# A two-layer trunk kernel: the causal mask of DeltaNet's decays written by transfers, GpSimd's powers read a step later, the first heads' gated rows beside the next units, and the first loads in another order

## The chip, the cores and the metric

The kernel runs on one core of one Trainium2 chip, as one launch. The metric is the device time of that core in microseconds (us), the median of several runs. TensorE is called PE here, VectorE DVE, ScalarE ACT, GpSimd POOL and SyncE SP, as in the profile; "SPq" and "POOLq" are the DMA issues of the last two.

## What is computed

The reference is a trunk of two layers over 256 tokens of width 1024, in fp32:

```python
# each layer
x = x + 0.5 * swiglu(rmsnorm(x, ffn1_norm), ffn1_w_in, ffn1_w_out)   # 1024 -> 2 x 2816 -> 1024
x = x + mixer(rmsnorm(x, mix_norm))      # layer 0: attention and RG-LRU; layer 1: DeltaNet
x = x + cross_attention(rmsnorm(x, xa_norm), rmsnorm(mem, xa_mem_norm), ...)
x = x + 0.5 * swiglu(rmsnorm(x, ffn2_norm), ffn2_w_in, ffn2_w_out)
# after both layers
out = rmsnorm(x, final_norm)

# the DeltaNet mixer, 8 heads of width 128, chunks of C = 64 tokens
qkv, z, a, b = split(h @ w_in)
q, k, v = split(silu(causal_dwconv(qkv, conv_w)))       # 4 taps
q, k = l2norm(q), l2norm(k)
beta = sigmoid(b);  g = -exp(a_log) * softplus(a + dt_bias)
gcum = cumsum(g)                                         # within a chunk
decay = exp(where(tril, gcum[i] - gcum[j], -inf))        # the causal mask of the decays
amat = I + strict_lower((k * beta) k^T * decay)          # inverted, then u, w, states and outputs
o = rmsnorm(chunked outputs, o_norm) * silu(z)
out = o @ w_out
```

The kernel works in chunks of 128 tokens, two of them, instead of 64.

## The kernel before

**Weights.** fp32 products are made of three fp32r products of high and low halves. All weights pass through one stream: `plan` lists units of 1024 (or fewer) rows by 256 columns, and `queue` lists their halves of four 128-row pieces, 512 KB each. `load_to` issues a half's DMA into one of five buffers `raw` (`RAW = 5`, SP's queue, L135). `split_half` makes the high half on ACT (L148, a copy to fp32r) and the low half on DVE (L149, a subtraction). `unit` multiplies: for each of 8 row pieces and two column halves `mm3` issues a high product of 512 columns (L190, both halves of the activations `x2`) and a low one of 256 (L194). A unit is thus 16 such pairs on PE. `unit` yields after each quarter and `run` or `fill` then calls `tick`, which splits the next half and runs what is due: `after(n, fn)` puts a step n ticks later. `w` issues loads until five halves beyond the last split one are under way. The order of the instructions on each engine then comes from the framework's scheduler, except in `manual_schedule` blocks, where it is the order of the code.

**Start (`setup`).** x is loaded in six DMAs into two of the five `raw` buffers (L462), in the order of its columns: 256, 256 and 512 columns, for both token halves each. Then come three halves of weights. PE turns x by transposes (`transposed`, L419, eight for each of two banks `psf` and `pss`, four 256-column pieces), and `take` makes the high half on ACT (L481) and the low on DVE (L484). The first norm's scale is not applied here but to the results of the first units (`times_bc`). The rows of `x` are squared on ACT (L492) and copied to `xT` on DVE (L494). `ffn` then runs the units of the first SwiGLU: the first unit goes to `gs`, the second to `us`, and so on; the first unit's 16 pairs need two halves of weights, and so do the second's.

**DeltaNet (`mixer1`).** The units of its input product run in the order of `DN_ORDER`: k, q, v and z of head pairs 0 to 3 (`k0` to `z3`), `K2` and `K3` being keys of the cross-attention. `conv` adds a unit's bank to `xn` (ACT L260, DVE L261: this frees the bank) and runs the taps on DVE (L1026); `silu` follows. `01|v3 z1` means that `back(0)` and `back(1)`, the inverse and the outputs of pairs 0 and 1, run in alternation with the units v3 and z1, `DN_FILL` telling after how many quarters.

The decays of pair p: `decay_rows` writes gcum to DRAM (POOL's DMA `gd<-gt`, L1010), `load` reads it into `e` on every partition (POOL's DMA `e<-gd`, L1068, four of 256 KB), `masked` adds on POOL the mask `neg_up` (`dn_negup`, -1e30 above the diagonal; L1072, four additions of 128x512), and `exp` is on ACT. `DEC = (2, 4, 4)` are the ticks of the three. `matrix` multiplies `kk`, `nb` and `e` to `na` on DVE (L1120), which goes to DRAM for the inversion (`store`, `invert`).

`sums` takes a norm's power of -0.5 on POOL (`rs_dn`, L331). `scales` then makes on DVE `nb_all` (L1098, from a reciprocal on DVE) and `hb_all` (L1099, from `rs_dn`), `products` makes `rq_all` (L1146, from `rs_dn`) and the decayed scores (L1150). `rq_all` is read in `back` alone and `hb_all` in the v units' rows.

At the end of a group `gated` multiplies each pair's outputs on DVE (L1286, four of 128x128; their norm is POOL's `ro`, then `ro_all` L1279), and `gated_T` turns them on PE (L1295) into `a2`, the input of the output product. In the first group this stands between the background units and `v2`.

## Time and profile before

| what | value |
|---|---|
| median of 3 runs | 1262.11 us (1261.82 to 1263.52) |
| the profiled execution | 1262.28 us, its span 1260.5 us |
| PE busy | 1240.2 us (98%) |
| DVE busy | 936.8 us (74%) |
| ACT busy | 748.9 us (59%) |
| POOL busy | 86.1 us (7%) |
| moved by DMA | 221.86 MB, 176 GB/s |

The span is that of the profiled core from its first to its last instruction; what lies around it is 1.8 us in this execution. "Busy" adds up instructions, so that the rest of PE's span, some 20 us, is time in which it waited or had nothing. Times of the timeline are counted from the span's start. The layer-1 DeltaNet mixer lies at about 795 to 910 us.

### The profile page before, as it was taken

The page shows a single profiled execution, that of the slowest core. Times are in us where ns is not written, and L with a number is a line of the kernel's source. Part 1 is how long each engine was busy: PE and PEld are TensorE (multiplying, and loading weights), DVE is VectorE, ACT ScalarE, POOL GpSimd, SP SyncE. Part 2 cuts the span into 40 slices and gives each one's busy share as a digit, 9 for nine tenths or more (in the row PEclk, how much of TensorE's full clock was granted, in tenths as well). Part 3 has the DMA queues.
Part 4 walks back from the last instruction along what each step waited for, and adds up shares of the span by engine and source line. Part 5 has one row for each costly group of instructions (what it writes and reads, how often), then busy time and mean ns, then how long its engine had stood idle before and what let it go on. Part 6 is the DMA issues. An engine that isn't in the chain of part 4 may idle for free.

```text
span 1260.5 us, 20362 instructions
## 1 busy us (share of the span) xinstructions
PE 1240.2 (98%) x7726; PEld 1107.8 (88%) x7726; DVE 936.8 (74%) x1595; ACT 748.9 (59%) x1274; POOL 86.1 (7%) x101
## 2 busy tenths in 40 slices
PE   7999999999999999999999999999999999999998
PEld 6888889888998888888888888888898998888887
DVE  6888866788668778766877756999757768777753
ACT  5766645876555665545655545775747555665543
POOL 1000020000101000011000001130001101000000
PEclk9999999999999999999999999999999999999999
DMA  7766585644545666567666555656533645666561
GB/s 231 234 209 194 183 253 184 182 151 133 185 134 153 187 195 186 174 192 232 185 187 184 190 184 176 176 161 174 138 102 105 196 134 155 186 195 185 178 194 63
DMA packets 228409, 221.86 MB, mean 176 GB/s; under 512 B 14920, under 2 KB 226008, under 8 KB 228184
## 3 DMA queue, kind: packets, MB, share of 16 engines
q1 hardware_dynamic: 227384, 217.42, 55.9%
q0 software_dynamic: 928, 3.15, 0.9%
q8 instruction: 60, 0.98, 0.3%
q14 instruction: 37, 0.30, 0.1%
HBM read 215.03 MB, written 5.51 MB: 175 GB/s over the span
## 4 chain that ended last, share of the span: by engine, by line
PE 74%; issue 17%; DVE 4%; DMA 2%; ACT 1%; POOL 1%; SPq 0%; POOLq 0%; DVEq 0%; ACTq 0%
PE psw L190 16%; PE pss L190 13%; PE psf L190 8%; PE psw L194 8%; PE pss L194 7%; PE psw L232 5%; PE psf L194 4%; PE psf L232 3%; PE pss L232 2%; PE psw L206 1%; DVE wt L149 1%; PE pss L1219 1%; PE psf L1227 1%; PE psw L210 1%; DVE y L1026 1%
## 5 line engine op out<-in xcount | busy, mean ns | idle before, releaser
L149 DVE TENSOR_TENSOR wt<-raw,wt 128x1024 fp32r<-128x1024 f32 (+1 forms) x406 | 484.9, 1198 | 201.7 <-ACT wt L148 199.3
L148 ACT ACTIVATE wt<-raw 128x1024 fp32r<-128x1024 f32 (+1 forms) x406 | 418.1, 1036 | 170.3 <-PE psw L194 57.1
L190 PE MATMUL psw<-x,wt 128*128 128x512 f32 x856 | 308.2, 396 | 3.2 <-DVE xn L261 3.0
L194 PE MATMUL psw<-x,wt 128*128 128x256 f32 x856 | 223.7, 282 | 0.0
L190 PE MATMUL pss<-x,wt 128*128 128x512 f32 x536 | 195.3, 396 | 1.9 <-ACT wt L148 1.9
L190 PEld LDWEIGHTS psw<-x,wt 128*128 128x128 f32 x856 | 159.2, 188 | 31.1 <-DVE xn L261 3.6
L194 PEld LDWEIGHTS psw<-x,wt 128*128 128x128 f32 x856 | 161.2, 189 | 8.5
L194 PE MATMUL pss<-x,wt 128*128 128x256 f32 x536 | 140.2, 282 | 0.5 <-DVE wt L149 0.5
L190 PE MATMUL psf<-x,wt 128*128 128x512 f32 x344 | 124.1, 393 | 0.0
L190 PEld LDWEIGHTS pss<-x,wt 128*128 128x128 f32 x536 | 101.3, 189 | 19.6 <-ACT wt L148 2.3
L194 PEld LDWEIGHTS pss<-x,wt 128*128 128x128 f32 x536 | 101.6, 190 | 6.3 <-DVE wt L149 1.0
L326 POOL TENSOR_TENSOR acc<-acc,sq 128x256 f32<-128x256 f32 x49 | 44.9, 916 | 658.8 <-ACT sq L324 658.5
L194 PE MATMUL psf<-x,wt 128*128 128x256 f32 x344 | 89.5, 281 | 0.0
L190 PE MATMUL pss<-h,wt 128*128 128x512 f32 x242 | 87.0, 397 | 0.0
L190 PE MATMUL psw<-h,wt 128*128 128x512 f32 x242 | 86.9, 396 | 0.0
L190 PEld LDWEIGHTS psf<-x,wt 128*128 128x128 f32 x344 | 64.6, 188 | 11.0
L194 PEld LDWEIGHTS psf<-x,wt 128*128 128x128 f32 x344 | 64.8, 188 | 3.8
L194 PE MATMUL pss<-h,wt 128*128 128x256 f32 x242 | 66.0, 280 | 0.0
L194 PE MATMUL psw<-h,wt 128*128 128x256 f32 x242 | 66.0, 280 | 0.0
L190 PE MATMUL psf<-h,wt 128*128 128x512 f32 x176 | 63.3, 397 | 0.0
L190 PEld LDWEIGHTS pss<-h,wt 128*128 128x128 f32 x242 | 45.5, 188 | 9.9
L190 PEld LDWEIGHTS psw<-h,wt 128*128 128x128 f32 x242 | 45.5, 188 | 9.9
(379 smaller groups left out, 2135.3 us busy)
## 6 DMA issues: line engine op xcount, KB each, us to landing
raw<-in_ffn_w_in_dram SPq DMA_DIRECT2D x176, 512.0 KB, 4.4
raw<-in_ffn_w_out_dram SPq DMA_DIRECT2D x80, 512.0 KB, 4.0
raw<-in_xa_wkv_dram SPq DMA_DIRECT2D x32, 512.0 KB, 3.9
raw<-in_dn_w_in_dram SPq DMA_DIRECT2D x32, 512.0 KB, 4.0
raw<-in_ab_w_in_dram SPq DMA_DIRECT2D x20, 512.0 KB, 4.5
raw<-in_xa_wq_dram SPq DMA_DIRECT2D x16, 512.0 KB, 3.5
raw<-in_xa_wo_dram SPq DMA_DIRECT2D x16, 512.0 KB, 3.6
raw<-in_ffn_w_out_dram SPq DMA_DIRECT2D x16, 256.0 KB, 2.8
```

The costliest lines, as they stand in the source:

```text
L148: nc.scalar.activation(a, r, AF.Copy)
L149: nc.vector.tensor_sub(b, r, a.bitcast(F32))
L190: nc.tensor.matmul(out.rearrange("p a s -> p (a s)"), w[:, 0, cols], mov[:, k].rearrange("p a s -> p (a s)"), start=k == start, stop=k == ...
L194: nc.tensor.matmul(out[:, 0], w[:, 1, cols], mov[:, k, 0], start=False, stop=False)
L206: nc.tensor.matmul(out.rearrange("p a s -> p (a s)"), mov[:, k, 0, tok], w.rearrange("p a s -> p (a s)"), start=k == 0, stop=k == KD - 1)
L210: nc.tensor.matmul(out[:, 0], mov[:, k, 1, tok], w[:, 0], start=False, stop=False)
L232: self.nc.tensor.matmul(out, a[u], b[w], start=first and i == 0, stop=last and i == 2)
L326: (eng or nc.gpsimd).tensor_add(self.acc, self.acc, sq)
L1026: nc.vector.scalar_tensor_tensor(y[:, j, d:], x[:, :S - d], tap(i), y[:, j, d:], op0=OP.mult, op1=OP.add)
L1219: nc.tensor.matmul(py[:, i], na[:, i], tu[:, 0, i], start=True, stop=True)
L1227: nc.tensor.matmul(pp[:, i], l[:, i], r[:, i], start=True, stop=True)
```

## The change

1. **Mask.** `masked` is gone. At tick 2 of the mixer (`MASK`), four DMAs on SP's queue copy `neg_up` into the four `e` buffers (256 KB each, from SBUF to SBUF), and POOL's four DMAs `e<-gd` add to what is there (`accum_op`). `DEC` is `(2, 4)`.
2. **Powers.** `hb_all` and `rq_all` are computed one tick later than `rs_dn`.
3. **Gated rows of pairs 0 and 1.** After the first group they are put 1 to 4 ticks into the next unit, `q2`. Unit v2 moves into the group's background, and one quarter of it runs before the first step of `back`.
4. **Start.** The second half of the first unit and the first half of the second change places in the queue of weights. x has a buffer of its own (`xs`), so that five halves can be loaded at once; its four DMAs stand around those of the first two halves of weights. PE gets 16 idle products of `ones` (7, 3 and 6). The products of both first units with the first half of x are issued before x's second half is turned; the rest comes after it. The first unit's halves of weights are split in two pieces each, and so is the second unit's second half.

On PE, the rows at the start of the program. Before (`ident,raw` are the transposes of x, `x_79` is `x2`, `wt` the split weights):

```order
L466 MATMUL psw<-ident,dcw 128x128
L419 MATMUL psf<-ident,raw 128x128 x4
L419 MATMUL pss<-ident,raw 128x128 x4
L419 MATMUL psf<-ident,raw 128x128 x4
L419 MATMUL pss<-ident,raw 128x128 x4
L190 MATMUL pss<-x_79,wt 128x512
L194 MATMUL pss<-x_79,wt 128x256
L190 MATMUL pss<-x_79,wt 128x512
```

All 16 transposes stand ahead of the first product. After, from the same place (`xs` is x's own buffer, `ones` the idle products' operand):

```order
L491 MATMUL psw<-ones 128x128 x7
L483 MATMUL psw<-ident,dcw 128x128
L429 MATMUL psf<-ident,xs 128x128 x4
L491 MATMUL psw<-ones 128x128 x3
L429 MATMUL pss<-ident,xs 128x128 x4
L491 MATMUL psw<-ones 128x128 x6
L200 MATMUL psw<-x_79,wt 128x512
L204 MATMUL psw<-x_79,wt 128x256
```

Eight transposes stand ahead of the first product now; the other eight come after eight pairs of products.

On POOL, the rows of the first decays in the DeltaNet mixer, where DVE waits for `rs_dn`. Before:

```order
L1010 DMA gd<-gt 16x128
L331 TENSOR_TENSOR rs_dn<-ss,mhalf 128x4
L1068 DMA e<-gd 128x512 x4
L1072 TENSOR_TENSOR e<-e,dn_negup 128x512
L331 TENSOR_TENSOR rs_dn<-ss,mhalf 128x4
L1072 TENSOR_TENSOR e<-e,dn_negup 128x512 x3
L331 TENSOR_TENSOR rs_dn<-ss,mhalf 128x4 x4
```

After:

```order
L1062 DMA gd<-gt 16x128
L341 TENSOR_TENSOR rs_dn<-ss,mhalf 128x4
L1123 DMA e<-gd 128x512 x4
L341 TENSOR_TENSOR rs_dn<-ss,mhalf 128x4 x5
L341 TENSOR_TENSOR ro<-so,mhalf 128x4 x2
```

The four additions are gone, and nothing stands between the DMAs and the next powers.

On DVE, the rows around the second pair's scales in the same place. Before:

```order
L1026 SCALAR_TENSOR_TENSOR y<-xn,dcw,y 128x254
L1098 TENSOR_TENSOR nb_all<-nbeta,r_8264 128x2x2
L1099 TENSOR_TENSOR hb_all<-ss,rs_dn 128x2x2
L1026 SCALAR_TENSOR_TENSOR y<-xn,dcw,y 128x253
L261 TENSOR_TENSOR xn<-psw,xn 128x256
L1120 SCALAR_TENSOR_TENSOR na<-psf,nb_all,e 128x128 x4
```

After:

```order
L1078 SCALAR_TENSOR_TENSOR y<-xn,dcw,y 128x254
L1150 TENSOR_TENSOR nb_all<-nbeta,r_8294 128x2x2
L271 TENSOR_TENSOR xn<-psw,xn 128x256
L1078 SCALAR_TENSOR_TENSOR y<-xn,dcw,y 128x253
L1151 TENSOR_TENSOR hb_all<-ss,rs_dn 128x2x2
L1172 SCALAR_TENSOR_TENSOR na<-psf,nb_all,e 128x128 x2
```

`xn`, which frees PE's bank, stands ahead of `hb_all` and of a tap now.

On DVE, the first group's gated rows. Before:

```order
L1267 TENSOR_TENSOR qk<-pss,q_8348 128x2x128
L1276 TENSOR_SCALAR so<-so 128x4
L1279 TENSOR_TENSOR ro_all<-ro,rq_all 128x2x2
L1286 SCALAR_TENSOR_TENSOR qk<-qk,ro_all,z 128x128 x4
L1276 TENSOR_SCALAR so<-so 128x4
L261 TENSOR_TENSOR xn<-psw,xn 128x256
L1279 TENSOR_TENSOR ro_all<-ro,rq_all 128x2x2
L1286 SCALAR_TENSOR_TENSOR qk<-qk,ro_all,z 128x128 x4
```

After:

```order
L1319 TENSOR_TENSOR qk<-pss,q_8375 128x2x128
L1078 SCALAR_TENSOR_TENSOR y<-xn,dcw,y 128x253
L1328 TENSOR_SCALAR so<-so 128x4
L1331 TENSOR_TENSOR ro_all<-ro,rq_all 128x2x2
L1338 SCALAR_TENSOR_TENSOR qk<-qk,ro_all,z 128x128 x4
L1328 TENSOR_SCALAR so<-so 128x4
L271 TENSOR_TENSOR xn<-psw,xn 128x256
L1331 TENSOR_TENSOR ro_all<-ro,rq_all 128x2x2
L1338 SCALAR_TENSOR_TENSOR qk<-qk,ro_all,z 128x128 x3
```

The multiplications stand in the same succession, with v2's taps ahead of them; on PE, a whole unit (q2) lies around their transposes where before the end of z1 did.

The diff, cut to its core:

```diff
 NEG = -1e30
-DN_ORDER = ('k0 k1 q0 q1 k2 v0 k3 v1 z0', '01|v3 z1', 'v2 q2 q3 z2', '23|z3 K2 K3')
-DN_FILL = ((1, 0, 1, 2, 0, 2, 1, 3, 2, 10, 1), (1, 0, 1, 0, 2, 1, 1, 0, 0, 5, 0))
+DN_ORDER = ('k0 k1 q0 q1 k2 v0 k3 v1 z0', '01|v3 z1 v2', 'q2 q3 z2', '23|z3 K2 K3')
+DN_FILL = ((1, 0, 1, 2, 0, 2, 1, 3, 2), (1, 0, 1, 0, 2, 1, 1, 0, 0, 5, 0))
...
 TWICE = 'k0 k1 q0 q1'.split()
-DEC = (2, 4, 4)
+DEC = (2, 4)
+MASK = 2
...
         self.queue = [(i, k) for i, u in enumerate(self.plan) for k in range(0, u[4], 4)]
+        self.queue[1], self.queue[2] = self.queue[2], self.queue[1]
...
             yield from ffn(2, l)
-    def load_to(self, n):
+    def load_to(self, n, step=4):
...
             src = self.t[name][l, (k0 + k) * P:(k0 + k + m) * P, c0:c0 + cols]
-            nc.sync.dma_start(raw[:, :m, :cols], src.rearrange("(k p) c -> p k c", p=P))
+            src = src.rearrange("(k p) c -> p k c", p=P)
+            for u in range(0, m, step):
+                us = slice(u, min(m, u + step))
+                nc.sync.dma_start(raw[:, us, :cols], src[:, us])
...
             self.n_load += 1
-    def split_half(self):
+    def split_half(self, step=4):
...
         wt = self.p_wt.tile([P, 4, 2, 256], F32R, name="wt")
-        a, b, r = wt[:, :n, 0, :cols], wt[:, :n, 1, :cols], self.raws.pop(self.n_half)[:, :n, :cols]
+        raw = self.raws.pop(self.n_half)
         self.n_half += 1
-        nc.scalar.activation(a, r, AF.Copy)
-        nc.vector.tensor_sub(b, r, a.bitcast(F32))
+        for u in range(0, n, step):
+            us = slice(u, min(n, u + step))
+            a, b, r = wt[:, us, 0, :cols], wt[:, us, 1, :cols], raw[:, us, :cols]
+            nc.scalar.activation(a, r, AF.Copy)
+            nc.vector.tensor_sub(b, r, a.bitcast(F32))
...
         nc.scalar.activation(warm, self.ones[:, :1], AF.Silu)
-        xs = [self.p_raw.tile([P, D], F32, name="raw") for _ in range(2)]
+        x_pool = tc.tile_pool(name="xs", bufs=1, reuse_waits="tile")
+        xs = x_pool.__enter__().tile([P, 2, D], F32, name="xs")
...
         put(rows0, 0, "ffn1_norm", nc.sync, times=8)
-        for a, b in ((0, 256), (256, 512), (512, 1024)):
-            for j in range(2):
-                nc.sync.dma_start(xs[j][:, a:b], x[:, j, a:b])
-        self.load_to(3)
+        for a, b in ((0, 256), (256, 512)):
+            nc.sync.dma_start(xs[:, :, a:b], x[:, :, a:b])
+        self.load_to(1, 2)
+        self.load_to(2)
+        for a, b in ((512, 768), (768, 1024)):
+            nc.sync.dma_start(xs[:, :, a:b], x[:, :, a:b])
+        self.load_to(RAW)
+        xs = [xs[:, j] for j in range(2)]
...
         with tc.manual_schedule():
+            def idle(n):
+                ps = self.bank("w").rearrange("p a s -> p (a s)")
+                for _ in range(n):
+                    nc.tensor.matmul(ps[:, :P], self.ones, self.ones, start=True, stop=True)
+            idle(7)
...
             def take(ks, ps):
-                if ks.start == 6:
-                    self.split_half()
...
                                                    op0=OP.mult, op1=OP.subtract)
-            self.transposed(xs, take)
+            self.first = [[self.bank(w) for w in u] for u in ("ww", "ws")]
+            def products(u, half, j):
+                self.mm3(self.first[u][j], self.halves[u], slice(j * P, j * P + P), self.x2,
+                         range(4 * half, 4 * half + 4))
+            self.transposed(xs, take, (0,))
+            idle(3)
+            self.transposed(xs, take, (1,))
+            idle(6)
+            self.split_half(2)
+            products(0, 0, 0)
             self.split_half()
+            products(0, 0, 1)
+            self.transposed(xs, take, (2, 3))
+            products(1, 0, 0)
+            products(1, 0, 1)
+            for u in range(2):
+                self.split_half(2)
+                for j in range(2):
+                    products(u, 1, j)
+            self.load_to(4 + RAW)
...
                 nc.vector.tensor_copy(self.xT[:, ks], ps)
+        x_pool.__exit__(None, None, None)
         self.acc, self.ms = None, ms
+        self.n_take = 2
...
                 us = hp.tile([P, 2, S], F32, name="us", bufs=2)
-                self.run(self.unit(f"ffn{i}_w_in", c * 256, mov, self.to(gs), lead=c == 0))
-                up = deque([self.unit(f"ffn{i}_w_in", FF + c * 256, mov, self.to(us))])
-                if c == 0:
+                if self.first:
+                    for dst, banks in zip((gs, us), self.first):
+                        for j, ps in enumerate(banks):
+                            self.to(dst)(j, ps)
+                    self.first, up = None, deque()
+                    self.stats_rows()
+                else:
+                    self.run(self.unit(f"ffn{i}_w_in", c * 256, mov, self.to(gs), lead=c == 0))
+                    up = deque([self.unit(f"ffn{i}_w_in", FF + c * 256, mov, self.to(us))])
+                if c == 0 and up:
...
                 e = four("e", EB)
+                def mask():
+                    nc.sync.dma_start(e, neg_up[:, None, :].to_broadcast([P, 4, P]))
...
                     nc.gpsimd.dma_start(e, bass.AP(tensor=gd.tensor, offset=gd.offset + 4 * p * P,
-                                                   ap=[[0, P], [1, 4 * P]]))
-                def masked():
-                    nc.gpsimd.tensor_add(e, e, neg_up[:, None, :].to_broadcast([P, 4, P]))
+                                                   ap=[[0, P], [1, 4 * P]]), accum_op=OP.add)
...
                     st[p]["e"] = e
-                d0, d1, d2 = DEC
+                d0, d1 = DEC
+                self.after(MASK, mask)
                 self.after(n + d0, load)
-                self.after(n + d1, masked)
-                self.after(n + d2, exp)
+                self.after(n + d1, exp)
...
                     nc.vector.tensor_mul(nb, nbeta[:, :, hs], r2)
-                    nc.vector.tensor_mul(hb, ss, r)
+                    self.after(1, lambda: nc.vector.tensor_mul(hb, ss, r))
...
                     ss, r = sums(s.pop("sq"), twice)
-                    nc.vector.tensor_scalar(rq_all[:, :, hs], r, -P ** -0.5, None, op0=OP.mult)
+                    self.after(1, lambda: nc.vector.tensor_scalar(rq_all[:, :, hs], r, -P ** -0.5, None, op0=OP.mult))
...
                     value_steps(c, y, twice)
-            assert AB[0] < AB[1] < AB[2] < min(AB[3:]) and DEC[0] < DEC[1] <= DEC[2]
+            assert AB[0] < AB[1] < AB[2] < min(AB[3:]) and DEC[0] < DEC[1]
...
                 parts = list(DN_FILL[i // 2])
+                if i == 1:
+                    self.fill(bg, 1)
...
                         self.fill(bg, parts.pop(0))
+                if i == 1:
+                    self.fill(bg)
+                    for n, p in enumerate(group):
+                        self.after(1 + n, lambda p=int(p): gated(p))
+                        self.after(3 + n, lambda p=int(p): gated_T(p))
+                    continue
...
                 for p in group:
```

## The prediction

> **What bounds the kernel now.** The page's first part comes first:
>
> ```profile
> span 1260.5 us, 20362 instructions
> PE 1240.2 (98%) x7726; PEld 1107.8 (88%) x7726; DVE 936.8 (74%) x1595; ACT 748.9 (59%) x1274; POOL 86.1 (7%) x101
> ```
>
> PE is the bound, and nothing in the change takes a product away. A gain can come only out of the 20.3 us in which PE isn't busy (1260.5 - 1240.2) and out of products at a low clock. The view of PE's waits lists these 20 us; the lines that the change can touch are:
>
> ```profile
> PE psw L466 <- DMA dcw<-in_ffn_norm_dram: 3.4, 1, 3.4
> PE psw L190 <- DVE xn L261: 3.0, 2, 1.5
> PE pss L190 <- ACT wt L148: 1.9, 1, 1.9
> PE pss L1295 <- DVE qk L1286: 1.6, 2, 1.3
> PE psf L419 <- DMA raw<-in_x_dram: 1.4, 3, 0.9
> PE pss L1219 <- DMA tu<-d: 0.5, 1, 0.5
> PE psw L206 <- DVE ti L1186: 0.3, 1, 0.3
> ```
>
> Two places hold them: the start (3.4 + 1.9 + 1.4) and the DeltaNet mixer (3.0 + 1.6 + 0.5 + 0.3 = 5.4).
>
> **Start.** The timeline of the first 26 us (start, duration, engine and line, tiles, in brackets the idle time and its releaser):
>
> ```profile
> 6.54 0.84 ACT L481 ACTIVATE x<-pss,bc 128x256 fp32r<-128x256 f32 x2 [0.40 <-PE pss L419]
> 7.41 0.88 DVE L484 SCALAR_TENSOR_TENSOR x<-pss,bc,x 128x256 fp32r<-128x256 f32 x2 [0.35 <-ACT x L481]
> 8.87 1.06 PE L419 MATMUL pss<-ident,raw 128*128 128x128 f32 x4
> 10.67 1.06 ACT L148 ACTIVATE wt<-raw 128x1024 fp32r<-128x1024 f32 x1 [0.72 <-DMA raw<-in_ffn_w_in_dram]
> 11.78 0.79 PE L190 MATMUL pss<-x,wt 128*128 128x512 f32 x1 [1.85 <-ACT wt L148]
> 14.06 0.63 PE L190 MATMUL pss<-x,wt 128*128 128x512 f32 x1
> 14.70 0.63 PE L190 MATMUL pss<-x,wt 128*128 128x512 f32 x1
> 14.82 0.68 DVE L494 COPY xT<-psf 128x512 f32<-128x512 f32 x1
> 16.42 0.40 PE L190 MATMUL psf<-x,wt 128*128 128x512 f32 x1
> 16.77 0.39 PE L190 MATMUL psf<-x,wt 128*128 128x512 f32 x1
> 22.15 1.22 DVE L149 TENSOR_TENSOR wt<-raw,wt 128x1024 fp32r<-128x1024 f32 x1
> 25.46 0.39 PE L190 MATMUL psf<-x,wt 128*128 128x512 f32 x1
> ```
>
> The first product waits until 11.78 for the first half of weights, whose DMA lands behind all of x. A pair takes 14.70 - 14.06 = 0.64 us at first and 16.77 - 16.42 = 0.35 later, so that the clock opens between 15.3 and 16.4. The third unit starts at 25.46; that is the mark, since everything behind it is a chain of units. The window of 5 to 11 us (its length, busy PE, PEld, DVE, ACT and POOL with their counts, clock, DMA share, GB/s) shows what the transfers do meanwhile:
>
> ```profile
> 5.00:11.00 6.00, 3.73 (x14) 2.22 (x12) 2.63 (x6) 2.84 (x7) 0.01 (x1) 1.00 0.89 294
> ```
>
> After: x's first half is turned and split as before (ACT ends at 6.54 + 0.84 = 7.38, DVE at 8.29). The first half of weights now stands behind 512 KB of x, not 1 MB. At those 294 GB/s 512 KB less are 1.8 us, and with half a tile to wait for another 0.9: it lands at about 10.6 - 2.7 = 7.9 or, at the rate of the first packets, a little sooner. Half a split is 0.53 on ACT and 0.61 on DVE (halves of the 1.06 and 1.22): first high product at 8.0 to 8.4, first low at about 9. Eight pairs on the first unit are bound by its second piece and end at about 11.6; eight transposes (1.06 for four, cold) give 12.5 to 13.7; 24 pairs at 0.35 are 8.4. That is 20.9 to 22 for the third unit (and 0.2 for the rows of the statistics), if DVE follows. DVE doesn't: x's last four low pieces (2 x 0.88) end at about 14.9, the two remaining splits (1.22 each) at about 17.3, and behind them it has four copies to `xT` (4 x 0.68, from 14.82 on in the row), four sums for `gs` and `us` (half as wide, an estimate of 4 x 0.34) and the 1.22 of the next half: 17.3 + 2.7 + 1.4 + 1.2 = 22.6. The third unit's low products start at about 22.5. Gain: 25.46 - 22.5 = 3.0. Against it: the sixth half of weights can be issued only when a buffer is free (-0.3), and the clock. The 16 idle products may open it before the real ones or not; if not, some four of the pairs until 12 take 0.64 and not 0.35, 1.4 us less. I take 2.0, in the middle between 3.0 - 0.3 = 2.7 and 2.7 - 1.4 = 1.3; ends 0 (as before) and 4.4 (25.46 - 21.1, were DVE no bound).
>
> The Trainium skill, page "TensorE: Matmul & The Clock Gate", Part 1, says that the clock opens after a window of about 3.4 us of activity; the 3.6 to 4.6 us from 11.78 agree. Part 4 says that transposes don't count for it, which speaks against an early opening, since eight of them stand between the idle products; by it the start would give 1.3 instead of 2.7.
>
> **The powers and the mask.** The timeline of the mixer:
>
> ```profile
> 811.68 0.46 DVE L1026 SCALAR_TENSOR_TENSOR y<-xn,dcw,y 128x253 f32<-128x253 f32 x1
> 813.68 0.17 DVE L1099 TENSOR_TENSOR hb_all<-ss,rs_dn 128x4 f32<-128x4 f32 x1 [0.85 <-POOL rs_dn L331]
> 814.25 2.25 POOL L1068 DMA_DIRECT2D e<-gd  x4 [0.60 <-DMA gd<-gt]
> 818.87 1.56 POOL L1072 TENSOR_TENSOR e<-e,dn_negup 128x512 f32<-128x512 f32 x1 [2.37 <-DMA e<-gd]
> 819.21 1.25 DVE L1098 TENSOR_TENSOR nb_all<-nbeta,r 128x4 f32<-128x4 f32 x1
> 820.46 1.28 ACT L1077 ACTIVATE e<-e,ngc 128x128 f32<-128x128 f32 x4 [2.40 <-POOL e L1072]
> 821.41 3.94 POOL L1072 TENSOR_TENSOR e<-e,dn_negup 128x512 f32<-128x512 f32 x3
> 821.46 1.26 DVE L1099 TENSOR_TENSOR hb_all<-ss,rs_dn 128x4 f32<-128x4 f32 x1 [1.01 <-POOL rs_dn L331]
> 822.65 1.56 DVE L1026 SCALAR_TENSOR_TENSOR y<-xn,dcw,y 128x253 f32<-128x253 f32 x1
> 824.60 0.50 PE L190 MATMUL psw<-x,wt 128*128 128x512 f32 x1 [1.46 <-DVE xn L261]
> 829.22 0.17 DVE L1146 TENSOR_SCALAR rq_all<-rs_dn 128x4 f32<-128x4 f32 x1 [0.87 <-POOL rs_dn L331]
> 830.97 0.50 PE L190 MATMUL psw<-x,wt 128*128 128x512 f32 x1 [1.52 <-DVE xn L261]
> ```
>
> While POOL adds the mask, DVE operations with two inputs in SBUF stand still: `nb_all` takes 1.25 and ends with the addition, `hb_all` 1.26 against 0.17 at 813.68, a tap 1.56 against 0.46. That is 1.08 + 1.09 + 1.10 = 3.3 us of DVE, and its waits for `rs_dn` before 824.60 are 0.85 + 1.01; the second of these stands behind POOL's first addition. (The Trainium skill, "SBUF — State Buffer", "Who interferes with whom", calls this an exclusive lock between GpSimd and DVE with two SBUF inputs; the three rows agree, and taking the mask off POOL frees them.) So DVE loses 3.3 + 1.01 = 4.3 us just before 824.60, where PE waits 1.46, and 0.87 more before 830.97, where PE waits 1.52. The 4.3 are more than both waits, and the rest of the backlog goes with it, so both go: 3.0. `xn` stands ahead of `hb_all` in the new order, which alone would save the first. Next late is nothing on DVE by a wait I can see, though it stays nearly full:
>
> ```profile
> 780.00:800.00 20.00, 19.78 (x115) 16.95 (x114) 18.09 (x40) 14.37 (x29) 0.64 (x1) 1.00 0.71 202
> 820.00:840.00 20.00, 17.02 (x110) 14.90 (x109) 17.87 (x37) 16.35 (x37) 7.72 (x7) 1.00 0.60 164
> ```
>
> In 820 to 840 DVE is busy 17.87, some 2.2 of it blocked time; v2's taps come only behind pair 0's inverse. Ends for both waits: 0 and 3.3.
>
> The four mask DMAs are 1.05 MB more on SP's queue early in the mixer, among the loads of `dn_w_in`. At 202 GB/s and a share of 0.71, the engines could carry 285 GB/s; 1.05 MB are 3.7 us of them and 20 x 0.29 = 5.8 are idle. The loads queued behind are late by at most 3.7, and the weights wait in their buffers for longer than that: no wait of ACT for `raw` stands in this stretch. Cost 0; without that cover, 3.7 us at most.
>
> The accumulating DMA has no row. The nearest are:
>
> ```profile
> e<-gd POOLq DMA_DIRECT2D x4, 256.0 KB, 6.0
> tu<-d SPq DMA_DIRECT2D x8, 256.0 KB, 3.9
> ```
>
> From 814.25 to 818.87 the first `e` took 4.6, the median is 6.0. Adding means reading the destination too: nothing extra if the engines hide it, 3.9 more if it costs a transfer of this size. ACT's `exp` (820.46) starts now when `e` lands, so that a first landing at up to 820.46 (1.6 later) costs nothing against before, and PE stood 2.8 us of DVE's backlog before it waited (4.3 late, 1.5 of wait). Up to about 4 us more is therefore nearly free. I take no loss. Removing the additions makes POOL free for `rs_dn` as well; POOL's queue has no other work there.
>
> **Gated rows.** The end of the first group:
>
> ```profile
> 895.77 1.14 DVE L1286 SCALAR_TENSOR_TENSOR qk<-qk,ro_all,z 128x128 f32<-128x128 f32 x4
> 896.27 0.30 PE L1295 MATMUL pss<-ident,qk 128*128 128x128 f32 x1 [1.28 <-DVE qk L1286]
> ```
>
> PE has run out of background here and waits 1.28 and 0.3 for a chain that goes from its last product over ACT and POOL's `ro` to DVE. With the 16 pairs of q2 (5.5 us) to run, the transposes come after they are ready, at least those of pair 0; the second pair's row stands 1.1 us behind the first. I take 1.1 of the 1.6, ends 0 and 1.6. v2's 5.5 us move from behind the group into it and cover the wait for `ti` (0.3); the wait for `tu` (0.5) is the end of a chain of DMAs that begins with `na`, which comes earlier by what DVE gains, and later by the `na` pieces that now stand behind taps: I leave it.
>
> **Sum.** 2.0 + 3.0 + 1.1 + 0.3 = 6.4. 1262.28 - 6.4 = 1255.9 for an execution like the profiled one; the median of the runs, 1262.11, lies 0.17 lower: 1255.7. The ends are 0 and 4.4 + 3.3 + 1.6 + 0.8 = 10.1.
>
> **Rivals.** 0.2%, or 2.5 us, is about what a measurement of this kernel can tell from no change.
> - The accumulating DMAs land so late that the mixer's gain is eaten. All four are issued in 2.25 us on one queue; if each pays a second transfer and they go one behind the other, the first is 4 and the last 8 or more late, and DVE's `na` blocks taps and `xn` behind it. The mixer gives 0 to 3 instead of 4.4: 1258 to 1261. For it speaks that `na` stands in DVE's order ahead of the `xn` that PE needs; against it the 4 us of slack.
> - The start gives nothing, because the clock opens as late as before or DVE's queue of copies and sums is the bound: 1257.7. For it: DVE's next split stands at 22.15 in the row above, and still has all its work ahead of it.
> - The tail: DVE, with v2's six taps added to the group, makes `tu` or the gated rows late instead: PE waits some 3 us there (six taps of 0.46), 1258.7. Against it, v2's own 5.5 us of PE stand there too, and hide more than the taps take.
>
> - Slower: the accumulation alone. An addition in the DMA that makes the landing 5 times as long (23 us for the first) holds `exp`, and with it ACT, whose splits and `xn` additions are queued behind. PE would wait about 23 - 4.6 - 1.6 - 2.8 = 14 there: 1262 - 6.4 + 14 = 1270. It ends on the slow side from a landing of about 4 times (18.4 - 4.6 - 1.6 - 2.8 = 9.4 of wait, less 6.4 of gain, is 3.0). The Trainium skill, "SBUF — State Buffer", "SBUF: two separate sides", has a trap in which descriptors of GpSimd's DMAs starve beside DVE and a DMA takes 5 times as long. The 4.6 us of the first `e`, beside a DVE that was hardly idle, do not show it, and an accumulation does not change who writes the descriptors.
>
> **Chances.** The forecast (1253 to 1258) 62%; the late accumulation 15%, of which 6 are faster by more than 2.5 us, 8 within it and 1 slower; the empty start 13%; the tail 5%; slower 5%. From these: faster by over 0.2% 0.62 + 0.13 + 0.05 + 0.06 = 0.86, within 0.08, slower 0.06. The range, 1251.5 to 1260, takes the forecast with its bounds, the start and the tail and half of the late accumulation.
>
> **What would show it.** The first real product at 8 to 8.5 and the third unit at 22 to 23.5; no idle time of PE before the products behind `xn` at 815 to 830; `nb_all`, `hb_all` at 0.17 and taps at 0.46 throughout; PE's transposes of gated rows without a wait over 0.5. Wrong would be: `exp` or `na` waiting for `e<-gd` by more than 4 us, ACT waiting for `raw` at 785 to 810, or pairs at 0.64 us beyond 15.

## The result and the profile after

The changed kernel takes 1255.99 us (median of 6 runs, 1255.27 to 1257.82) against 1262.95 (median of 6, 1261.82 to 1263.52): ratio 0.9946, 95% interval 0.9936 to 0.9956, 6.8 us by the ratio. The profiled executions stand at 1255.88 and 1262.28 us with spans of 1254.1 and 1260.5: 6.4 us in both ways of counting. The page's first part and the view of PE's waits:

```profile
span 1254.1 us, 20430 instructions
PE 1242.4 (99%) x7758; PEld 1110.8 (89%) x7758; DVE 933.5 (74%) x1598; ACT 749.8 (60%) x1277; POOL 83.1 (7%) x97
```

```profile
PE psw L200 <- DVE xn L271: 1.1, 1, 1.1
PE psw L491 <- DVE mhalf L452: 1.1, 1, 1.1
PE pss L1271 <- DMA tu<-d: 0.4, 1, 0.4
PE pss L1347 <- DVE qk L1338: 0.3, 1, 0.3
```

The long waits at the start are gone (3.4, 1.9 and 1.4 before), the two for `xn` have become one of 1.1, the ones for the gated rows fell from 1.6 to 0.3, and `ti` is no longer in the list. To part start and mixer, a mark is needed between them: two small products of the layer's statistics just before the mixer, at 780.70 us before and here in the changed kernel:

```profile
777.63 0.43 PE L374 MATMUL pss<-ident,rcol 128*128 128x128 f32 x2 [0.21 <-POOL rcol L341]
```

Between these two profiles 3.1 us are saved ahead of the mark and 3.3 behind it (479.8 to 476.5). The start in the timeline:

```profile
1.05 3.36 PE L491 MATMUL psw<-ones 128*128 128x128 f32 x14 [1.05 <-DVE mhalf L452]
4.96 0.98 PE L429 MATMUL psf<-ident,xs 128*128 128x128 f32 x4 [0.35 <-DMA xs<-in_x_dram]
5.78 0.83 PE L491 MATMUL psw<-ones 128*128 128x128 f32 x6
8.49 0.50 PE L200 MATMUL psw<-x,wt 128*128 128x512 f32 x1
10.41 0.39 PE L200 MATMUL psw<-x,wt 128*128 128x512 f32 x1
10.76 0.39 PE L200 MATMUL psw<-x,wt 128*128 128x512 f32 x1
13.65 0.88 DVE L506 SCALAR_TENSOR_TENSOR x<-psf,bc,x 128x256 fp32r<-128x256 f32 x2 [1.69 <-ACT x L503]
21.59 1.22 DVE L159 TENSOR_TENSOR wt<-raw,wt 128x1024 fp32r<-128x1024 f32 x1
21.70 0.48 PE L200 MATMUL pss<-x,wt 128*128 128x512 f32 x1
23.09 0.28 PE L204 MATMUL pss<-x,wt 128*128 128x256 f32 x1
```

The first seven idle products are 14 rows of the profile, two each, and take 0.24 us a row (3.36 for 14); the next three take 0.14 from 5.78 on (0.83 for 6). The clock is open then, and the first real pairs stand 0.35 apart (10.41 and 10.76). The third unit's first high product is at 21.70 instead of 25.46, but its first low product only at 23.09, behind DVE's split at 21.59. PE issues high products ahead of the low ones in that time, and some 0.7 us of the 3.8 (25.46 - 21.70) is given back before the fifth unit (36.77 before, 33.66 now). The mixer:

```profile
811.16 3.63 POOL L1123 DMA_DIRECT2D e<-gd  x4 [0.58 <-issue]
816.13 0.16 DVE L1150 TENSOR_TENSOR nb_all<-nbeta,r 128x4 f32<-128x4 f32 x1
816.53 1.28 ACT L1129 ACTIVATE e<-e,ngc 128x128 f32<-128x128 f32 x4 [1.54 <-DMA e<-gd]
816.54 0.47 DVE L1078 SCALAR_TENSOR_TENSOR y<-xn,dcw,y 128x253 f32<-128x253 f32 x1
816.93 0.16 DVE L1151 TENSOR_TENSOR hb_all<-ss,rs_dn 128x4 f32<-128x4 f32 x1
822.04 1.28 ACT L1129 ACTIVATE e<-e,ngc 128x128 f32<-128x128 f32 x4 [1.70 <-DMA e<-gd]
823.75 1.26 ACT L1129 ACTIVATE e<-e,ngc 128x128 f32<-128x128 f32 x4
824.92 0.36 ACT L270 ACTIVATE xn<-psw 128x256 f32<-128x256 f32 x1
825.31 0.42 DVE L271 TENSOR_TENSOR xn<-psw,xn 128x256 f32<-128x256 f32 x1 [0.23 <-ACT xn L270]
```

`nb_all`, `hb_all` and the taps are back at 0.16 and 0.47. What is new is ACT's wait for the accumulating transfers: 1.54 and 1.70. ACT's half of `xn` stands in its queue behind the exponentials at 822.04 and 823.75, so that `xn` is ready at 825.7 and PE, which wants its bank, waits 1.1. The groups of DMA issues say why (size, and the median time to landing):

```profile
e<-gd POOLq DMA_DIRECT2D x4, 256.0 KB, 8.4
```

The median to landing went from 6.0 to 8.4 us.

### The profile page after: what moved, and what is told of

Its sections match the earlier page's. It is cut to its first block, busy times and chain, and to the rows that moved or that the text cites. A ratio compares the mean times of both kernels' runs of the same rounds, so it can differ in the third digit from the quotient of the medians.

```text
span 1254.1 us, 20430 instructions
## 1 busy us (share of the span) xinstructions
PE 1242.4 (99%) x7758; PEld 1110.8 (89%) x7758; DVE 933.5 (74%) x1598; ACT 749.8 (60%) x1277; POOL 83.1 (7%) x97
## 4 chain that ended last, share of the span: by engine, by line
PE 75%; issue 18%; DVE 3%; ACT 2%; DMA 2%; POOL 0%; SPq 0%; POOLq 0%; DVEq 0%; ACTq 0%
PE psw L200 17%; PE pss L200 12%; PE psw L204 9%; PE psf L200 8%; PE pss L204 6%; PE psw L242 4%; PE psf L204 4%; PE psf L242 3%; PE pss L242 2%; PE psw L216 1%; DVE wt L159 1%; PE pss L1271 1%; PE psf L1279 1%; DMA e<-gd 1%; PE psw L220 1%
## 5 line engine op out<-in xcount | busy, mean ns | idle before, releaser
L200 PE MATMUL psw<-x,wt 128*128 128x512 f32 x864 | 311.4, 396 | 1.4 <-DVE xn L271 1.1
L200 PE MATMUL pss<-x,wt 128*128 128x512 f32 x520 | 188.0, 394 | 0.1
L204 PE MATMUL pss<-x,wt 128*128 128x256 f32 x520 | 135.3, 281 | 0.0
L200 PE MATMUL psf<-x,wt 128*128 128x512 f32 x352 | 127.5, 394 | 0.0
L200 PEld LDWEIGHTS pss<-x,wt 128*128 128x128 f32 x520 | 97.6, 188 | 17.0 <-ACT bc L377 0.4
L204 PEld LDWEIGHTS pss<-x,wt 128*128 128x128 f32 x520 | 97.9, 188 | 5.4
L200 PE MATMUL psw<-h,wt 128*128 128x512 f32 x264 | 94.9, 396 | 0.0
L200 PEld LDWEIGHTS psf<-x,wt 128*128 128x128 f32 x352 | 66.1, 188 | 11.2
L204 PE MATMUL psw<-h,wt 128*128 128x256 f32 x264 | 72.0, 280 | 0.0
L204 PEld LDWEIGHTS psf<-x,wt 128*128 128x128 f32 x352 | 66.3, 188 | 3.5
L200 PEld LDWEIGHTS psw<-h,wt 128*128 128x128 f32 x264 | 49.6, 188 | 10.8
L200 PE MATMUL psf<-h,wt 128*128 128x512 f32 x154 | 55.4, 397 | 0.0
```

The lines of the kernel that those rows point to most:

```text
L200: nc.tensor.matmul(out.rearrange("p a s -> p (a s)"), w[:, 0, cols], mov[:, k].rearrange("p a s -> p (a s)"), start=k == start, stop=k == ...
L204: nc.tensor.matmul(out[:, 0], w[:, 1, cols], mov[:, k, 0], start=False, stop=False)
```

## The experiments

The start varies by itself: in the ten profiles with the new start and its idle products, the mark lies between 777.06 and 778.94 us. It goes roughly with the first real product, which stands between 7.77 and 10.02 us in them. So the profiles are read as mark and rest (span less mark), and each time stands beside its ratio:

| kernel | median us | ratio to before, 95% | mark | rest |
|---|---|---|---|---|
| before | 1262.95 | | 780.70 | 479.8 |
| changed | 1255.99 | 0.9936 to 0.9956 | 777.63 | 476.5 |
| start alone | 1258.62 | 0.9951 to 0.9976 | 777.88 | 479.2 |
| mixer alone | 1259.34 | 0.9956 to 0.9981 | 781.70 | 476.2 |
| no idle products | 1256.70 | 0.9935 to 0.9963 | 778.75 | 476.1 |
| plain transfers | 1255.00 | 0.9927 to 0.9952 | 777.52 | 475.5 |
| mask on POOL | 1257.77 | 0.9944 to 0.9971 | 778.94 | 478.2 |
| powers at once | 1257.55 | 0.9947 to 0.9972 | 777.19 | 477.7 |
| gated as before | 1256.74 | 0.9935 to 0.9960 | 777.06 | 476.9 |
| pair 1 second | 1257.56 | 0.9943 to 0.9968 | 778.41 | 476.7 |
| pair 1 second, 2 and 3 late | 1255.70 | 0.9933 to 0.9959 | 777.33 | 476.2 |
| pairs 2 and 3 late | 1260.80 | 0.9970 to 0.9988 | 777.60 | 481.3 |
| the same, all a tick earlier | 1256.96 | 0.9941 to 0.9966 | 777.56 | 478.7 |

Three profiles have the whole changed mixer (changed, mixer alone, no idle products). Their rests are 476.1 to 476.5, so that differences of the rest under 0.5 us say nothing. Where PE waits differs among them too, with the same code in the mixer (for `xn`, then for `tu`): 1.14 and 0.43 in the changed kernel, 0.32 and 1.04 with the mixer alone, nothing and 1.04 without the idle products:

```profile
PE pss L1220 <- DMA tu<-d: 1.0, 2, 0.8
PE psw L191 <- DVE xn L262: 0.3, 1, 0.3
```

```profile
PE pss L1271 <- DMA tu<-d: 1.0, 2, 0.6
```

The first fence is of the mixer alone, the second of the kernel without the idle products. One profile thus doesn't tell which of the two waits an edit has removed.

The ten marks have a mean of 777.7; the two of the old start, 780.70 and 781.70, have 781.2, so that the start's gain is 3.5 us by the means. The single profiles stand for the other executions too: the median span of all executions of a kernel less the mean mark gives the rest of the table within 0.2 us for eight of the ten. For "pair 1 second" it gives 477.8 instead of 476.7 and for "the same, all a tick earlier" 477.4 instead of 478.7, so that these two rests are uncertain by over 1 us.

Each ratio is against runs of the kernel before on the same chip, whose medians were 1262.94 to 1263.25.

**The start alone**, the kernel before with part 4:

```diff
 # part 4 of the change as it is; in the mixer:
 # DN_ORDER, DN_FILL, DEC and masked() as before, hb_all and rq_all at once, gated() and gated_T() behind the group
```

> The kernel before with part 4 (the start) alone. Theory: the start gives what the changed kernel's trace shows at equal places behind it, 3.1 us, independent of the rest: 1262.95 - 3.1 = 1259.9, with the mixer's waits for xn (1.46 and 1.52) and for the gated rows (1.28) as before. Rival: the gain at the start is partly taken back where the mixer meets its loads earlier, and less than 2 us is left: above 1261.

Measured 0.9964 (0.9951 to 0.9976, so 3.0 to 6.2 us), and 2.8 us at the mark. The mixer's waits are those of before (the view of PE's waits):

```profile
PE psw L199 <- DVE xn L270: 3.0, 2, 1.5
PE pss L1346 <- DVE qk L1337: 1.6, 2, 1.3
```

The start's gain stays, and the rival, by which less than 2 us is left, falls.

**The mixer alone**, the kernel before with the changed `mixer1` and its tables:

```diff
-DEC = (2, 4, 4)
+DEC = (2, 4)
+MASK = 2
 # and mixer1, DN_ORDER and DN_FILL of the changed kernel
```

> The kernel before with parts 1 to 3 (the mixer) alone. Theory: 3.3 us, so 1259.6, with one wait for xn of about 1.1 us left, 0.3 to 0.4 for the gated rows and 0.4 for tu. Rival: the parts depend on the start (its loads leave the queue in another order), and the mixer gives under 2 or over 4.5 us.

Measured 0.9968 (0.9956 to 0.9981, 2.4 to 5.6 us), and 3.6 us in the rest. The gains at mark and rest, 2.8 and 3.6, add up to the 6.4 of the whole, but a mark is not sure to 1 us; by the ratios the parts are 4.5 and 4.0 us against 6.8, each uncertain by some 1.6. So the parts may be independent, and these runs don't show it closer than that. The wait for `xn` was 0.32 us in this execution and not 1.1.

**Without the idle products**:

```diff
-                for _ in range(n):
+                for _ in range(0):
                     nc.tensor.matmul(ps[:, :P], self.ones, self.ones, start=True, stop=True)
```

> The changed kernel without the 16 idle products. Theory: they open the clock at 5.7 us, ahead of the first real product; without them the first pairs from 8.5 take 0.64 instead of 0.35 us for about 3.9 us, six pairs, and the eight transposes take 0.21 each: 1.8 us more, 1257.8. Rival one: DVE's splits, copies and sums are the bound at the start, so that nothing is lost: 1256.0. Rival two: the transposes of x open the clock by themselves: 1256.0 as well, but with pairs at 0.35 from 10 us on.

The timeline at the start:

```profile
5.93 1.11 PE L429 MATMUL pss<-ident,xs 128*128 128x128 f32 x4 [0.47 <-DMA xs<-in_x_dram]
8.50 0.79 PE L200 MATMUL psw<-x,wt 128*128 128x512 f32 x1 [1.45 <-ACT wt L158]
10.51 0.63 PE L200 MATMUL psw<-x,wt 128*128 128x512 f32 x1
11.15 0.63 PE L200 MATMUL psw<-x,wt 128*128 128x512 f32 x1
14.87 0.88 DVE L506 SCALAR_TENSOR_TENSOR x<-psf,bc,x 128x256 fp32r<-128x256 f32 x2 [3.22 <-ACT x L503]
22.82 1.22 DVE L159 TENSOR_TENSOR wt<-raw,wt 128x1024 fp32r<-128x1024 f32 x1
```

The first product stands at the same 8.50, and its pairs are 0.64 apart until 12.2. From the first product to the third unit it is 14.43 us (8.50 to 22.93) against 13.21 (8.49 to 21.70): the idle products are worth 1.2 us. The theory had 1.8, by six cold pairs and cold transposes: there are four to five such pairs at 0.29 more each, and x's second half is turned when the clock is open. Rival two falls, since the clock was low behind the eight transposes. Rival one falls too, though DVE is nearly always busy from the low pieces of x's second half on: that chain starts behind the first eight pairs, at 14.87 instead of 13.65, and the split of the third unit comes 1.23 us later with it (22.82 instead of 21.59). By the medians alone (0.7 us apart, with intervals of 2.5 and 3.5 us) none of this would be seen.

**Plain transfers**. This kernel leaves the mask out, so it only prices the accumulation:

```diff
-                                                   ap=[[0, P], [1, 4 * P]]), accum_op=OP.add)
+                                                   ap=[[0, P], [1, 4 * P]]))
...
-                            nc.scalar.activation(e[:, 2 * j + c], e[:, 2 * j + c], AF.Exp,
-                                                 bias=ngc[:, c, 2 * p + j:2 * p + j + 1])
+                            nc.scalar.activation(e[:, 2 * j + c], e[:, 2 * j + c], AF.Exp, scale=0.0,
+                                                 bias=gc[:, c, 2 * p + j:2 * p + j + 1])
```

> The changed kernel with its e<-gd transfers plain instead of accumulating; the mask's transfers stay but are overwritten, so the mask is left out, and the exponentials take a scale of 0 and another bias to keep the numbers finite (same instructions, same sizes). Theory: the landings of the four transfers go from 5.4, 7.2, 9.6 and 10.4 us after their issue back to 4.6 to 6.8, the exponentials no longer hold ACT, and the wait for xn (1.1 us) goes: 1254.9. Rival: the wait comes from DVE's order (na ahead of xn), not from the landing, and stays: 1256.0.

Its groups of DMA issues and its timeline:

```profile
e<-gd POOLq DMA_DIRECT2D x4, 256.0 KB, 6.1
```

```profile
822.10 0.36 ACT L270 ACTIVATE xn<-psw 128x256 f32<-128x256 f32 x1
```

The median to landing is 6.1 us and not 8.4 (the four: 3.6, 5.2, 7.0 and 7.1, against 5.4, 7.2, 9.6 and 10.4); `xn` on ACT at 822.10, 2.8 us earlier than in the changed kernel with the mark at an equal place, and no wait of PE for `xn`. The rest is 475.5: accumulation costs 1.0 us against the changed kernel's profile, 0.6 to 1.0 against the three. On DVE two `na` stand ahead of this `xn` and two behind it, as in the changed kernel, so the rival falls. But the wait for `tu` doubled from 0.4 to 0.8.

**The mask on GpSimd again**:

```diff
-DEC = (2, 4)
-MASK = 2
+DEC = (2, 4, 4)
...
-                self.after(MASK, mask)
                 self.after(n + d0, load)
+                self.after(n + d1, masked)
```

> The changed kernel with the mask added on GpSimd again (part 1 undone), powers still read a tick later. Theory: POOL's additions lock DVE's operations with two inputs (nb_all, hb_all or taps beside them at 1.2 to 1.6 us instead of 0.17 to 0.48), some 3 us of DVE; but plain transfers land earlier. PE waits for xn 1.5 to 3 us in all instead of 1.1: 1256.5 to 1258. Rival: what cost time before was DVE's wait for rs_dn in POOL's queue, which the later reading removes alone; then nothing is lost, or 1 us is gained with the plain transfers: 1255 to 1256.

```profile
817.03 1.50 DVE L1077 SCALAR_TENSOR_TENSOR y<-xn,dcw,y 128x254 f32<-128x254 f32 x1
819.40 3.95 POOL L1123 TENSOR_TENSOR e<-e,dn_negup 128x512 f32<-128x512 f32 x3
819.45 1.26 DVE L1150 TENSOR_TENSOR hb_all<-ss,rs_dn 128x4 f32<-128x4 f32 x1
822.14 2.30 DVE L158 TENSOR_TENSOR wt<-raw,wt 128x1024 fp32r<-128x1024 f32 x1
828.30 0.72 PE L199 MATMUL psw<-x,wt 128*128 128x512 f32 x1 [2.37 <-DVE xn L270]
829.03 0.63 PE L199 MATMUL psw<-x,wt 128*128 128x512 f32 x1
```

Beside POOL's additions a tap takes 1.50, `hb_all` 1.26, and even a split of weights 2.30 instead of 1.2. PE waits 2.37 us for `xn`, though the `hb_all` ahead of it doesn't wait for `rs_dn` any more (from 812 to 832 us DVE waits for a power once, 0.87 for `rq_all`). The rest is 478.2, 1.7 to 2.1 more, as the theory has it, but not by the wait alone: behind it the clock is low, and pairs are 0.64 apart from 828.30 to 831.6, which loses some 1.4 us (five pairs). So the additions on POOL are a cost of their own, and the queue of powers isn't all. In the kernel before, PE waited twice instead, 1.5 us each, with the clock at full.

**The powers at once**:

```diff
-                    self.after(1, lambda: nc.vector.tensor_mul(hb, ss, r))
+                    nc.vector.tensor_mul(hb, ss, r)
...
-                    self.after(1, lambda: nc.vector.tensor_scalar(rq_all[:, :, hs], r, -P ** -0.5, None, op0=OP.mult))
+                    nc.vector.tensor_scalar(rq_all[:, :, hs], r, -P ** -0.5, None, op0=OP.mult)
```

> The changed kernel with hb_all and rq_all computed at once after rs_dn is asked for (part 2 undone). Theory: with POOL free, rs_dn takes 1.0 us and DVE waits 0.85 once per power, eight times, of which PE sees only where DVE is late already, around 820 to 830: 0.3 to 1 us more, 1256.3 to 1257. Rival: the deferral is the part that moves xn ahead of hb_all and gives most of the mixer's gain: 1258 or more.

```profile
PE psw L216 <- DVE tm L1236: 1.5, 2, 1.1
PE psw L200 <- DVE xn L271: 1.4, 2, 1.2
```

```profile
843.15 0.17 DVE L1151 TENSOR_TENSOR hb_all<-ss,rs_dn 128x4 f32<-128x4 f32 x1 [0.92 <-POOL rs_dn L341]
```

The rest is 1.2 to 1.6 us longer, above the theory's 0.3 to 1 and below the rival. The cost lies where it was not looked for: DVE's wait of 0.92 at 843.15 stands amid the steps of the inverse, and behind it PE waits 1.5 us in all for `tm`; around 820 to 831 it is 0.3 more than in the changed kernel, and the wait for `tu` is no longer in the list.

**The gated rows as before**:

```diff
-DN_ORDER = ('k0 k1 q0 q1 k2 v0 k3 v1 z0', '01|v3 z1 v2', 'q2 q3 z2', '23|z3 K2 K3')
+DN_ORDER = ('k0 k1 q0 q1 k2 v0 k3 v1 z0', '01|v3 z1', 'v2 q2 q3 z2', '23|z3 K2 K3')
 # and DN_FILL, gated() and gated_T() as before
```

> The changed kernel with the gated rows, v2 and the filling as before (part 3 undone). Theory: the waits for the gated rows come back (1.28 + 0.28 against 0.29 + 0.11) and perhaps the 0.3 for ti: 1.2 to 1.5 us more, 1257.3. Rival: v2 beside the first group costs DVE more there than the rows give, so that undoing it changes nothing: 1256.

```profile
PE pss L1347 <- DVE qk L1338: 1.6, 2, 1.3
```

The waits are back to 1.6, 1.2 us more than in the changed kernel, yet the rest grows by only 0.4 to 0.9. The wait for `ti` did not come back. So the measured cost lies between theory and rival. What offsets the remainder is smaller than these runs resolve.

**The transfers' order and ACT's.** The last four runs try to remove the wait that the accumulation left.

```diff
-AB = (3, 5, 8, 10, 13, 12, 12)
+AB = (3, 5, 8, 10, 11, 12, 12)          # pair 1 second
...
-                self.after(n + d1, exp)
+                self.after(n + d1 + (6 if p > 1 else 0), exp)   # pairs 2 and 3 late
```

The first edit alone:

> The changed kernel with pair 1's decays asked for at tick 11 instead of 13, ahead of those of pairs 2 and 3 at 12 (one number in AB). In the changed kernel pair 1's e, which DVE needs next, is the last of the four to land, and ACT's exponentials wait for each in turn. Theory: pair 1's e lands as second, its na stand earlier in DVE, but the exponentials of pairs 2 and 3 still hold ACT until 822 ahead of the xn that PE needs: the wait for xn stays at 0.5 to 1.1; 1255.3 to 1256. Rival: it was na behind pair 1's late e that held xn in DVE's order: the wait goes, 1254.9.

```profile
826.00 0.50 PE L200 MATMUL psw<-x,wt 128*128 128x512 f32 x1 [0.56 <-DVE xn L271]
```

Half of the wait stays in this profile, though three of pair 1's four `na` are done by 823.7: DVE waits 1.84 for ACT's `xn`, which stands behind the last pair's exponential, as the theory has it. But the wait for `tu` is 0.8 here, and the median, 1257.56, lies above both theory and rival, so that the size is open. With both edits:

> The changed kernel with pair 1's decays at tick 11 (ahead of those of pairs 2 and 3) and the exponentials of pairs 2 and 3 six ticks later. Theory: in the first seven runs PE's wait for xn follows the exponential on ACT that waits for the accumulating transfers; with pairs 2 and 3 off ACT's way until they have long landed, xn stands ahead of them and the wait goes. From the mark in front of the mixer to the end 475.5 us, as with plain transfers, and not 476.5; by the median about 1255.0. Rival: DVE is the bound (18 of 20 us busy), and na's earlier rows or the later exponentials make another wait of the same size (for tu, or for xn at 828 to 832): 476.5, 1256.

```profile
863.71 1.13 PE L1279 MATMUL pss<-yy,tu 128*128 128x128 f32 x8 [1.05 <-DMA tu<-d]
```

The wait for `xn` is gone, and PE waits 1.05 for `tu` instead. The rest is 476.2, the ratio 0.9946: nearer the rival, though not clear of the theory. Pair 1's last `na` stands at the same place in DVE's time, and goes out at 825.88 (826.28 in the changed kernel), so that the inverse behind it isn't earlier. That the edits removed the wait isn't shown, though: the run without idle products has none of them, and it too has no wait for `xn`, 1.04 for `tu` and a rest of 476.1. The second edit alone:

> The changed kernel with the exponentials of pairs 2 and 3 six ticks later, pair 1's decays still asked for last. Theory: pair 1's e still lands last, at 10 us after the first issue, and its exponential still stands ahead of xn on ACT: the wait for xn stays at 1 us, 476.5 us from the mark, 1256. Rival: two exponentials less ahead of xn (2.6 us of ACT) are what counts: the wait goes, 475.5.

```profile
823.36 1.28 ACT L1129 ACTIVATE e<-e,ngc 128x128 f32<-128x128 f32 x4 [4.34 <-DMA e<-gd]
826.55 0.58 PE L204 MATMUL psw<-x,wt 128*128 128x256 f32 x1 [3.10 <-DVE wt L159]
826.93 0.63 PE L200 MATMUL psw<-x,wt 128*128 128x512 f32 x1
831.92 0.39 PE L200 MATMUL psw<-x,wt 128*128 128x512 f32 x1
```

```profile
820.00:840.00 20.00, 16.90 (x100) 15.02 (x98) 13.71 (x32) 15.14 (x34) 2.42 (x2) 0.83 0.62 169
```

Neither came: the rest is 481.3. ACT now stands 4.34 us at pair 1's exponential, as its `e` is the last to land, with a split and `xn` behind it. PE waits 3.10, and then runs its pairs at 0.64 us until 831.8; the window of 820 to 840 us (second fence) has a clock of 0.83. The theory had ACT's wait at pair 1's exponential right, but PE waits for the split `wt` and not for `xn`, and the size was wrong by 4.8 us. And both edits with everything a tick earlier (`AB` is `(2, 4, 7, 9, 10, 11, 11)`):

> As the run with pair 1 second and the exponentials of pairs 2 and 3 late, and with betas, decays and their transfers one tick (some 1.4 us) earlier. Theory: the landing of e for pairs 0 and 1 is then ahead of ACT, and neither the wait for xn nor the one for tu is left over 0.3 us: 475.0 us from the mark, 1254.6. Rival: the chain to the inverse does not hang on e any more, and the earlier small operations only push DVE's other work: 475.5 to 476.5.

```profile
820.68 1.05 PE L1107 MATMUL pss<-ones,th 128*128 128x1 f32 x8 [0.91 <-ACT th L1101]
823.37 0.63 PE L200 MATMUL psw<-x,wt 128*128 128x512 f32 x1
```

The rest is 478.7 in this profile and 477.4 by the median span, worse than its rival either way. ACT now waits for the first `e` by 2.8 us ahead of other work, and PE for ACT at 820.7 (0.91) and 836.9 (0.54). Behind the first of these waits stand eight products of one column, and behind them the clock is low until 825.3. No version that computes the whole beats the changed kernel beyond the interval.

## Why the prediction was right

The forecast of 1255.7 lies 0.3 us from the median, and its gain of 6.4 us stands against 6.8 measured. That it lies so close is luck: two of its terms were off by 1.1 us each, in opposite directions.

- **Start, 2.0 forecast, 3.1 measured** (2.8 by the run of the start alone, 3.5 by the means of the marks). The first product, said for 8.0 to 8.4, came at 8.49, one draw out of 7.77 to 10.02. The open-clock case was the true one, and its 2.7 would have been the better choice. The hedge for a low clock was the step that failed: the idle products opened it at 5.8 us, across the transposes. (Its four pairs of 0.29 are 1.2 us and not 1.4; the run without idle products lost 1.2.) By the rule that transposes don't count, from the Trainium skill's page "TensorE: Matmul & The Clock Gate", Part 4, the start would give 1.3; the trace agrees with the rule (without the idle products the clock stayed low behind the transposes, until 12.2) and not with what I drew from it, as seven idle products, 3.4 us of them, stood ahead of the first transposes of x. DVE as the bound was right from the low pieces of x's second half on (13.65): copies, sums and then the split at 21.59, low products at 23.09 where 22.5 was said. The third unit's first high product, at 21.70, came ahead of the 22 to 23.5 that were to show it.
- **Mixer, 4.4 forecast, 3.3 measured** (3.6 by the mixer alone). Of the two waits for `xn`, 1.1 of 3.0 stayed in this profile (0.3 and nothing in the two others with the same mixer, with a longer wait for `tu`). The step that failed is the price of the accumulation, put at nothing within 4 us of slack; by the run with plain transfers it is 0.6 to 1.0 us. The four land 1.8 to 3.3 us later after their issue than plain ones, as the bounds allowed, but the slack was counted for the first `e` alone. In this profile the exponentials of the last two stand ahead of ACT's half of `xn`, and ACT waits 1.70 us for the third to land. The late landing is the first rival's; its path is not, since the rival had DVE's `na` in the way, and its size of 1.4 to 4.4 was too large.
- **The lock of DVE beside POOL's additions** was right, and the mask's move is worth 1.7 to 2.1 us even with the powers put off. The low clock behind PE's wait, some 1.4 us there, is a cost that the working didn't have. The powers' move is worth 1.2 to 1.6 by itself, and the waits that come without it lie mostly at the inverse.
- **Mask transfers at no cost**: no wait of ACT for `raw` appears from 772 to 830 us, so this was right as far as it shows; no run leaves out these transfers alone.
- **Gated rows, 1.1 of 1.6**: the waits fell by 1.2, but the rest shows 0.4 to 0.9. `ti`'s 0.3 went, but hardly by v2's move, since it didn't come back when that was undone, and `tu`'s 0.5, which was left out of the sum, stayed at 0.4 in this profile. So the tail rival didn't come, nor did the empty start.
- **The slow rival** did not come, yet the run with pairs 2 and 3 late shows its path: ACT held by one `e`, PE by ACT. A wait of 4.34 us on ACT cost 4.8 us there, in part because the clock was low behind it. The rival's delay was far longer, some 18 us.

## What to carry to other kernels

Before work is moved from an engine to transfers, look at what stands in the queue behind the instruction that waits for the last of them, not the first: here ACT's exponentials, with an unrelated bank's release behind. Where several waits lie close together, less of one can mean more of the next (`xn`, then `tu`), even from one execution of the same code to another. So the time from a fixed mark to the end, held against the other executions, tells more than the list of waits. A few idle products while the first loads are under way were worth 1.2 us here: they opened the clock ahead of the first real product, which came no later for them (8.49 and 8.50).

## What the hardware showed that was not expected

- In three runs a wait in the middle of the program cost more than itself, since the clock was low behind it: 3.10 us of wait were followed by 5.3 us of pairs at 0.64 instead of 0.35, 2.37 us by 3.3, and 0.91 us with eight one-column products behind it by 2.7. The waits of 1.46 and 1.52 us before, and of 1.14 in the changed kernel, left it at full. What else decides this, above all in the third case, no run separates.
- An accumulating transfer of 256 KB lands 1.8 to 3.3 us later than a plain one (median 8.4 against 6.1 us to landing). Its four issues on POOL span 3.63 us against 2.25.
- DVE's 128x1024 subtraction of weights, both inputs in SBUF, takes 2.30 us beside a POOL addition instead of 1.2.
